# Seven block products instead of eight in the second MLP product of a decoder layer

## The chip, the cores and the metric

The kernel runs on one core of one Trainium2 chip. The core has a matrix engine (TensorE, PE in the profile), a vector engine (VectorE, DVE), a scalar engine (ScalarE, ACT), GpSimd (POOL), and SyncE (SP), whose queue issues nearly all DMA transfers here. The metric is the device time of one execution in microseconds (us). The kernel before takes 924.64 us (median of three runs, 924.51 to 924.73).

## The reference

One layer with two parallel mixers (windowed attention, RWKV-7), a merge, a normalization, and an MLP. All is float32, with 512 tokens of width 1024 after 16 meta tokens are cut off. What matters here are the last lines, where `w_ff1` is 1024 x 4096 and `w_ff2` is 4096 x 1024:

```python
        merged = jax.nn.sigmoid(gate_att) * att + jax.nn.sigmoid(gate_rwkv) * rw
        h = layer_norm(ALPHA * h + merged @ w_out[l], ln1_g[l], ln1_b[l])
        ff = jnp.square(jax.nn.relu(h @ w_ff1[l])) @ w_ff2[l]
        h = layer_norm(ALPHA * h + ff, ln2_g[l], ln2_b[l])
    return h[:, N_META:]
```

## The kernel before

Every float32 product is made of three products of a shorter float type (float32r). An operand is split into `hi`, its rounded copy (a ScalarE cast), and `lo`, the rest (a VectorE subtraction). The three are hi·hi, hi·lo and lo·hi, summed in the same PSUM bank (`three`, L498; `add` in `project`, L1607).

Everything up to the first normalization, and the first three of the 32 up products, is recorded in a plan and issued in a hand-written order of numbers (`ORDER`). The change leaves that order as it is. From L1585 on a scheduler orders the rest by priorities: the code's order counts, but a weight's load, cast and subtraction are moved ahead of it (`load`, L482, `ahead(100)`).

The MLP works on 32 hidden tiles of 128 rows, in two halves of 16 (L1653):

- **Up.** For tile f, `up` (L1664) takes a weight tile of 128 x 1024 (512 KB), splits it into `whi` and `wlo` (L476, L479), and runs 24 matmuls of 512 columns into one PSUM bank: 8 contraction tiles times 3. Their moving operands are the normalized rows `h1hi` and `h1lo`, one row of 512 tokens for each contraction tile. `up_evict` (L1657) makes the ReLU and the square on ScalarE (L1659, L1660), the square once more on VectorE (L1661), and its rest `flo` there too (L1662).
- **Down.** `project` (L1602) is called twice in each half, for output columns 0 to 511 and 512 to 1023. It runs over 16 contraction tiles and 4 blocks of 128 tokens; the stationary operand is a slice of `fhi` or `flo`, the moving one a half of `whi` or `wlo` of 512 columns. Over both halves this is 32 x 4 x 2 x 3 = 768 matmuls. After each call four sums go from PSUM into the residual tiles `res` (L1691).
- **Residual.** `res` holds the normalized rows and is multiplied by `ln1_g` and shifted by `ln1_b` along the way (L1683, eight instructions each, while the up products run).
- **End.** In the last call the four token blocks end one after the other. Each block's sum, statistics (L1631, L1639), root (POOL, L466), two passes of the normalization for each half of the columns (L1598, L1599) and output DMAs (L1647) follow at once; the first half of the columns was added, and its statistics taken, a call earlier.

Of the kernel before, what the change touches and what calls it, by code (L numbers as in the profile page):

```python
# [11 lines left out]
F32 = mybir.dt.float32  # L12
# [71 lines left out]
PRI = {"load": 100}  # L84
HOLD = 4
# [3 lines left out]
SUBST = 1  # L89

# [291 lines left out]
def hybrid_layer_kernel(ctx: ExitStack, tc: tile.TileContext, I: dict, out: bass.AP):  # L382
# [15 lines left out]
    @contextmanager  # L398
    def ahead(n):

        now = tc.cur_priority
        tc.cur_priority = now - n
        yield
        tc.cur_priority += n

# [62 lines left out]

    def split(raw, hi=None, lo=None, n=P):
        if hi is None:  # L470
            hi = wst.tile([P, D], F32R, name="whi", tag="whi", bufs=WB[0])
            lo = wst.tile([P, D], F32R, name="wlo", tag="wlo", bufs=WB[1])
        w = D // 2
        for q in range(2):
            qs = slice(q * w, (q + 1) * w)
            act.copy(hi[:n, qs], raw[:n, qs])  # L476
        for q in range(2):
            qs = slice(q * w, (q + 1) * w)
            dve.tensor_tensor(lo[:n, qs], raw[:n, qs], hi[:n, qs].bitcast(F32), op=ALU.subtract)  # L479
        return hi, lo  # L480

    def load(tiles, i, keep=None):  # L482

        with ahead(PRI["load"]):
            raw = wst.tile([P, D], F32, name="wraw", tag="wraw", bufs=WB[2])
            nc.sync.dma_start(raw, I[tiles][i])
            if keep is None:
                return split(raw)
            return split(
                raw, *(keep.tile([P, D], F32R, name="wk", tag="wk", bufs=2 * (HOLD - 2)) for _ in "hl")  # L490
            )

# [1091 lines left out]
    region.__exit__(None, None, None)  # L1584
    p2.close()  # L1585
    p1.close()
    h1hi, h1lo, fin = fin["hi"], fin["lo"], fin["pool"]
    rp = ctx.enter_context(tc.tile_pool(name="rp", bufs=1, side="right"))
    ffp = ctx.enter_context(tc.tile_pool(name="ffp", bufs=1))

    def rowvec(name, pool_=rp, tag=None):
        t = pool_.tile([P, D], F32, name="rv" + name, tag=tag or "rv" + name[-1], bufs=WB[2] if tag else 1)
        src = I["rows"][ROW0[name] : ROW0[name] + KT].rearrange("(a r) p -> a (r p)", a=1)
        nc.sync.dma_start(t, src.to_broadcast([P, D]))
        return t

    def norm_rows(t, mean, r, g_, b_):
        dve.scalar_tensor_tensor(t, t, mean, g_, op0=ALU.subtract, op1=ALU.mult)  # L1598
        dve.scalar_tensor_tensor(t, t, r, b_, op0=ALU.mult, op1=ALU.add)  # L1599

    res = [[rest_[b, n].t[:, :SEQ] for n in range(2)] for b in range(4)]
    def project(k0, nk, xhi, xlo, n, hold=2, more=None):  # L1602


        acc = [pa.tile([P, 512], F32, name=f"acc{b}", tag=f"acc{b}") for b in range(4)]

        def add(w, q, b):  # L1607
            hi, lo = w
            bs = slice(b * P, (b + 1) * P)
            for d in range(2):  # L1610
                k = q + d
                ws = slice(d * 512, (d + 1) * 512)
                first, last = k == 0, k == nk - 1
                pe.matmul(acc[b], xhi[:, k, bs], hi[:, ws], start=first, stop=False)  # L1614
                pe.matmul(acc[b], xhi[:, k, bs], lo[:, ws], start=False, stop=False)  # L1615
                pe.matmul(acc[b], xlo[:, k, bs], hi[:, ws], start=False, stop=last)  # L1616

        for q in range(0, nk - 2 * hold, 2):
            w = load("w_ff2", k0 + q + n)
            for b in range(4):  # L1620
                add(w, q, b)

        ends = range(nk - 2 * hold, nk, 2)
        ws = [load("w_ff2", k0 + q + n, more if d < hold - 2 else None) for d, q in enumerate(ends)]
        for b in range(4):
            for w, q in zip(ws, ends):
                add(w, q, b)
        return acc

    def half_stats(st, b, n):  # L1630
        dve.bn_stats(st[b][:, n, :], res[b][n])  # L1631

    def stats_tiles():
        return [rp.tile([P, 2, 6], F32, name=f"gst{b}") for b in range(4)]

    def moments(st, b):

        mv = rp.tile([P, 2], F32, name=f"gmv{b}")
        dve.bn_aggr(mv, st[b].rearrange("p a b -> p (a b)"))  # L1639
        return mv[:, 0:1], rstd_of(rp, mv, P, LN_EPS, f"f{b}")  # L1640

    def finish(b):
        mean, r = moments(st2, b)
        for q in range(2):
            qs = slice(q * 512, (q + 1) * 512)
            norm_rows(res[b][q], mean, r, g2[:, qs], b2[:, qs])
            (nc.sync, nc.scalar)[q].dma_start(out[0, b * P : (b + 1) * P, qs], res[b][q])  # L1647

    NF = DFF // P // 2
    taken = [home[id(u.t)] for u in ups]  # L1650
    turn_of = taken + [b for b in banks if b not in taken]
    turn_of = turn_of[: SPLITF] + sorted(turn_of[SPLITF:], key=lambda b: b[0] is pa)[:4]
    for half in range(2):  # L1653
        fhi = ffp.tile([P, NF, SEQ], F32R, name="fhi", tag="fhi")
        flo = ffp.tile([P, NF, SEQ], F32R, name="flo", tag="flo")

        def up_evict(f, ps):  # L1657
            r = rp.tile([P, SEQ], F32, name="rl", tag="rl", bufs=2)
            act.activation(r, ps, AF.Relu)  # L1659
            act.activation(fhi[:, f], r, AF.Square)  # L1660
            dve.tensor_tensor(r, r, r, op=ALU.mult)  # L1661
            dve.tensor_tensor(flo[:, f], r, fhi[:, f].bitcast(F32), op=ALU.subtract)  # L1662

        def up(f, w):  # L1664
            hi, lo = w
            pool_, tag = turn_of[f % len(turn_of)] if half == 0 else (pb, f"acc{f % 4}")
            ps = pool_.tile([P, 512], F32, name="dps", tag=tag)
# [3 lines left out]
            up_evict(f, ps)  # L1671

        split_f = SPLITF if half == 0 else 0
        for f in range(split_f):
            up_evict(f, ups[f].t)
        for f in range(split_f, NF):
            up(f, load("w_ff1", half * NF + f))
            if half == 0 and f in (6, 10):

                gb_ = rowvec(("ln1_g", "ln1_b")[f // 10], wst, "wraw")  # L1680
                for b in range(4):
                    for n in range(2):
                        dve.tensor_tensor(res[b][n], res[b][n], gb_[:, n * 512 : (n + 1) * 512], op=(ALU.mult, ALU.add)[f // 10])  # L1683
        if half == 0:
            g2, b2 = rowvec("ln2_g"), rowvec("ln2_b")
            st2 = stats_tiles()
        for n in range(2):
            ns = slice(n * 512, (n + 1) * 512)
            acc = project(half * NF, NF, fhi, flo, n, HOLD if half and n else 2, ffp)
# [61 lines left out]
```

## Time and profile before

| | before |
|---|---|
| median of three runs | 924.64 us (924.51 to 924.73) |
| profiled execution, first to last instruction (span) | 922.6 us |
| what the runs have around a span like that (924.64 - 922.6) | 2.0 us |
| TensorE busy | 98% of the span, 6496 matmuls |
| weight loads of TensorE | 84% |
| VectorE / ScalarE / GpSimd busy | 63% / 49% / 27% |
| DMA, mean | 104 GB/s |

The page of the profile gives busy times, the busy share in 40 slices of the span, the chain of work that ended last, and groups of equal instructions with the mean duration of one and the idle time ahead of them. A matmul's shown duration is longer than its distance to the next one, since they overlap; what a row of matmuls costs is read from the starts. The timeline lists instructions by start; "x2" means two equal ones that follow each other, with the time from the first start to the last end.

### The profile page before, as it was taken

How to read it: one execution, taken by the hardware profiler on the slowest of the kernel's cores; microseconds unless marked ns; L12 is line 12 of the kernel's file. 1: busy time of each engine (PE TensorE's matmuls, PEld its weight loads, DVE VectorE, ACT ScalarE, POOL GpSimd, SP SyncE). 2: the span in 40 equal slices, each digit the busy share in tenths (PEclk: the TensorE clock that was granted, in tenths of full speed). 3: DMA queues.
4: the chain of work that ended last, by engine and by line, in shares of the span. 5: the costliest groups of instructions: out<-in, count | busy, mean ns of one | idle time of the engine just before them, and what ended most of it. 6: DMA issues, size and time to landing. Idle time of an engine off the chain costs nothing. (4 is left out here: it accounts for less than half of the span.)

```text
span 922.6 us, 17014 instructions
## 1 busy us (share of the span) xinstructions
PE 902.2 (98%) x6496; PEld 773.6 (84%) x6496; DVE 585.8 (63%) x1141; ACT 456.3 (49%) x1080; POOL 245.6 (27%) x652
## 2 busy tenths in 40 slices
PE   7999999999999999999999999999999999999996
PEld 6999989888998888978878878888888888888885
DVE  7873977868777696587685887864323244442437
ACT  7845568476583664656637448434312234431120
POOL 4147173381634605507537020000000000000001
PEclk9999999999999999999989999999999999999999
DMA  7443323425242242313246322532223232233322
GB/s 265 125 131 99 93 84 101 111 67 127 72 110 86 68 141 69 83 54 114 64 140 182 100 92 69 172 126 92 92 91 107 76 114 92 91 93 98 100 75 92
DMA packets 71370, 95.90 MB, mean 104 GB/s; under 512 B 40071, under 2 KB 47497, under 8 KB 71289
## 3 DMA queue, kind: packets, MB, share of 16 engines
q1 hardware_dynamic: 70448, 93.65, 33.5%
q8 instruction: 51, 0.84, 0.4%
q10 hardware_dynamic: 840, 1.17, 0.3%
q14 instruction: 31, 0.25, 0.1%
HBM read 87.64 MB, written 8.21 MB: 104 GB/s over the span
## 5 line engine op out<-in xcount | busy, mean ns | idle before, releaser
L499 PE MATMUL g<-hhi,whi 128*128 128x512 f32 (+3 forms) x640 | 213.1, 333 | 0.2
L500 PE MATMUL g<-hlo,whi 128*128 128x512 f32 (+3 forms) x640 | 204.1, 319 | 1.7 <-DVE hlo L862 1.7
L501 PE MATMUL g<-hhi,wlo 128*128 128x512 f32 (+3 forms) x640 | 203.6, 318 | 0.0
L476 ACT CAST whi<-wraw 128x512 fp32r<-128x512 f32 x118 | 67.4, 619 | 205.7 <-PE acc L1616 107.4
L479 DVE TENSOR_TENSOR wlo<-wraw,whi 128x512 fp32r<-128x512 f32 x118 | 76.4, 689 | 144.5 <-ACT whi L476 141.7
L499 PEld LDWEIGHTS g<-hhi,whi 128*128 128x128 f32 x640 | 121.0, 189 | 12.6 <-issue 2.2
L500 PEld LDWEIGHTS g<-hlo,whi 128*128 128x128 f32 x640 | 121.2, 189 | 9.7 <-DVE hlo L862 2.1
L501 PEld LDWEIGHTS g<-hhi,wlo 128*128 128x128 f32 x640 | 121.0, 189 | 8.5 <-DVE wlo L658 0.2
L658 DVE TENSOR_TENSOR wlo<-wraw,whi 128x512 fp32r<-128x512 f32 x126 | 88.3, 708 | 30.4 <-ACT whi L656 29.8
L1167 POOL TENSOR_TENSOR ftmp<-Xf,Nf 108x84 f32<-108x84 f32 (+23 forms) x248 | 88.1, 355 | 73.4 <-DMA Nf<-Nd 44.7
L656 ACT CAST whi<-wraw 128x512 fp32r<-128x512 f32 x126 | 76.9, 618 | 55.5 <-PE g L500 23.5
L466 POOL TENSOR_TENSOR rsf<-rsf,mhalf 128x1 f32<-128x1 f32 x4 | 3.9, 964 | 348.5 <-DVE rsf L465 348.5
L1171 POOL TENSOR_TENSOR Xf<-Xf,ftmp 108x84 f32<-108x84 f32 (+23 forms) x248 | 88.5, 357 | 19.0
L1615 PE MATMUL acc<-wlo,fhi 128*128 128x512 f32 x240 | 93.4, 389 | 0.0
L1614 PE MATMUL acc<-whi,fhi 128*128 128x512 f32 x240 | 93.4, 389 | 0.0
L1616 PE MATMUL acc<-whi,flo 128*128 128x512 f32 x240 | 93.4, 389 | 0.0
L501 PE MATMUL dps<-h1hi,wlo 128*128 128x512 f32 x232 | 91.6, 395 | 0.0
L499 PE MATMUL dps<-h1hi,whi 128*128 128x512 f32 x232 | 91.6, 395 | 0.0
L500 PE MATMUL dps<-h1lo,whi 128*128 128x512 f32 x232 | 91.6, 395 | 0.0
L1614 PEld LDWEIGHTS acc<-whi,fhi 128*128 128x128 f32 x240 | 45.0, 188 | 9.5
L1616 PEld LDWEIGHTS acc<-whi,flo 128*128 128x128 f32 x240 | 45.0, 188 | 9.3
L1615 PEld LDWEIGHTS acc<-wlo,fhi 128*128 128x128 f32 x240 | 45.0, 188 | 9.3
(361 smaller groups left out, 1658.4 us busy)
## 6 DMA issues: line engine op xcount, KB each, us to landing
wraw<-in_w_ff_dram SPq DMA_DIRECT2D x64, 512.0 KB
wraw<-in_w_in_dram SPq DMA_DIRECT2D x52, 512.0 KB
wraw<-in_w_out_dram SPq DMA_DIRECT2D x14, 256.0 KB
Nf<-Nd SPq DMA_DIRECT2D x24, 144.0 KB
res<-in_x_dram SPq DMA_DIRECT2D x4, 512.0 KB
G<-in_consts_dram SPq DMA_DIRECT2D x16, 128.0 KB
XB<-xtd SPq DMA_DIRECT2D x16, 128.0 KB
res<-in_x_dram SPq DMA_DIRECT2D x8, 256.0 KB
```

What stands on the lines that cost most here:

```text
L476: act.copy(hi[:n, qs], raw[:n, qs])
L479: dve.tensor_tensor(lo[:n, qs], raw[:n, qs], hi[:n, qs].bitcast(F32), op=ALU.subtract)
L499: pe.matmul(ps, whi, xhi, start=first, stop=False)
L500: pe.matmul(ps, whi, xlo, start=False, stop=False)
L501: pe.matmul(ps, wlo, xhi, start=False, stop=last)
L656: AC(512, lambda hi=hi, qs=qs: act.copy(hi.t, raw.t[:, qs]), plain=True, r=[raw], w=[hi], new=[hi])
L658: f = lambda hi=hi, lo=lo, qs=qs, e=e: e.tensor_tensor(lo.t, raw.t[:, qs], hi.t.bitcast(F32), op=ALU.subtract)
L1167: sub(nj * nt, lambda s=s, nj=nj, nt=nt, tv=tv: pool.tensor_tensor(tv(), Xf.t[:, 0:nj, s : s + 1].to_broadcast([NB, nj, nt]), Nf.t[:, s : ...
L1171: sub(nj * nt, lambda s=s, nj=nj, tv=tv: pool.tensor_tensor(Xf.t[:, 0:nj, s + 1 :], Xf.t[:, 0:nj, s + 1 :], tv(), op=ALU.add), port=1, r=[ ...
L1614: pe.matmul(acc[b], xhi[:, k, bs], hi[:, ws], start=first, stop=False)
L1615: pe.matmul(acc[b], xhi[:, k, bs], lo[:, ws], start=False, stop=False)
L1616: pe.matmul(acc[b], xlo[:, k, bs], hi[:, ws], start=False, stop=last)
```

## The change

The second MLP product is cut into four groups of 8 hidden tiles. In three of them (24 of the 32 tiles, 12 of 16 pairs) each group is a 2 x 2 times 2 x 2 product of blocks: tokens 0 to 255 or 256 to 511 (t), even or odd tiles of the group (x), and output columns 0 to 511 or 512 to 1023 (d). Instead of eight block products of 24 matmuls there are seven, with sums of weight blocks and differences of activation blocks made on VectorE; several products go on in the same two PSUM banks (a chain, R, T or P), and after each the chain's present value is added to or taken from a quarter of `res`. The last group keeps eight products, in eight units.

The order is now the code's own, for the whole MLP. The list of units alternates one up product and one of the seven, and the last group's units end it. For unit i the loads are issued four units ahead, the splits (`prep`) two units ahead, then its matmuls, then its follow-up (`post`). The three up products of the plan are evicted ahead of the first unit. The square is made by VectorE alone, in place, and split when it is used. `res` gets the factor ALPHA with `ln1_g` and `ln1_b` in two lots of eight VectorE instructions, behind units 2 and 3. `finish` takes both halves' statistics at the end. A pad is 128 B longer: `h1hi` and `h1lo` began 128 B past a multiple of 512 B, and now begin at one. The weights of the second product lie in host memory in quarters of 1 MB, and one quarter of each of the three groups is loaded twice.

```diff
-        fin["pad"] = p.tile([P, 88], F32, name="fpad")
+        fin["pad"] = p.tile([P, 120], F32, name="fpad")
...
+    def finish(b, g2, b2):
+        for n in range(2):
+            dve.bn_stats(st2[b][:, n, :], res[b][n])
...
+        for q in range(2):
+            qs = slice(q * 512, (q + 1) * 512)
+            dve.scalar_tensor_tensor(res[b][q], res[b][q], mv[:, 0:1], g2[:, qs], op0=ALU.subtract, op1=ALU.mult)
+            dve.scalar_tensor_tensor(res[b][q], res[b][q], r, b2[:, qs], op0=ALU.mult, op1=ALU.add)
+            (nc.sync, nc.scalar)[q].dma_start(out[0, b * P : (b + 1) * P, qs], res[b][q])
...
+    bank_of = {"u": free[:2], "R": free[2:4], "P": [free[4], taken[0]], "T": taken[1:3]}
...
+        pool_, n = {"w": (wst, WB[0]), "b": (mp, 3), "a": (mp, 2)}[kind]
+        return tuple(pool_.tile([P, D], F32R, name=kind + q, tag=kind + q, bufs=n) for q in ("hi", "lo"))
...
+    def up_evict(f, ps):
+        t = ff_of(f // NF)[:, f % NF]
+        act.activation(t, ps, AF.Relu)
+        dve.tensor_tensor(t, t, t, op=ALU.mult)
...
+    def split_left(src):
+        hi, lo = pair_of("a")
+        v = lambda t: t.rearrange("p (i c) -> p i c", c=256)
+        act.copy(v(hi), src)
+        dve.tensor_tensor(v(lo), src, v(hi).bitcast(F32), op=ALU.subtract)
+        return hi, lo
+
+    def split_right(t):
+        out = []
+        for c in range(NP // 2):
+            hi, lo = pair_of("bw"[c % 2])
...
+    def products(left, right, acc, bs, first, last, again=False):
+        (ahi, alo) = left
+        for b in bs:
+            for i in range(NP):
+                bhi, blo = right[i // 2]
+                as_ = slice(i * 256 + b * P, i * 256 + (b + 1) * P)
+                ws = slice((i % 2) * 512, (i % 2 + 1) * 512)
+                for q, (l, r) in enumerate(((ahi, bhi), (ahi, blo), (alo, bhi))):
+                    pe.matmul(acc[b], l[:, as_], r[:, ws], start=first and i == 0 and q == 0,
+                              stop=last and i == NP - 1 and q == 2, skip_group_check=True)
...
+    def down(g, n):
+        left, chain, updates = (
+            ((1, 0),                 "R", (2, 0, ALU.add)),
+            (((1, 1), (1, 0)), "T", (2, 0, ALU.add)),
+            (((0, 1), (1, 0)), "R", (2, 1, ALU.subtract)),
+            ((0, 1),                 "P", (0, 1, ALU.add)),
+            (((1, 0), (0, 0)), "R", (0, 1, ALU.subtract)),
+            (((1, 1), (0, 1)), "P", (2, 1, ALU.add)),
+            (((0, 0), (0, 1)), "R", (0, 0, ALU.add)),
+        )[n]
+        first = n in (0, 1, 3)
+        loads = [[load_raw(g, 0, 0), load_raw(g, 1, 0)], [], [load_raw(g, 0, 1)], [load_raw(g, 1, 1)], [], [], [load_raw(g, 0, 0)]][n]
...
+            if n == 0:
+                chains["sum"] = plus(x0, y0)
+            elif n == 2:
+                plus(chains["sum"], x1)
+            elif n == 3:
+                plus(chains["sum"], y1)
+            elif n == 6:
+                plus(x0, x1)
+            right = (chains["sum"], y0, chains["sum"], chains["sum"], x1, y1, x0)[n]
+            if isinstance(left[0], tuple):
+                src = mp.tile([P, NP, 256], F32, name="dif", tag="dif", bufs=2)
+                dve.tensor_tensor(src, block_of(g, *left[0]), block_of(g, *left[1]), op=ALU.subtract)
...
+            s["r"] = split_right(right)
+            s["l"] = split_left(src)
...
+        def post():
+            b, d, op = updates
+            for i in range(2):
+                dve.tensor_tensor(res[b + i][d], res[b + i][d], chains[chain][i], op=op)
...
+        return [
+            unit(0, 0, (0,), both, [load_raw(g, 0, 0), load_raw(g, 0, 1)], [(0, 0)], [(0, 0)]),
+            unit(1, 0, (0,), both, [load_raw(g, 1, 0), load_raw(g, 1, 1)], [(1, 0)]),
...
+            unit(0, 1, both, (0,), (), [(0, 1)], [(1, 0)], done(0, 0)),
+            unit(0, 1, both, (1,), (), [], (), done(0, 1)),
+            unit(1, 1, both, (0,), (), [(1, 1)], (), done(1, 0)),
+            unit(1, 1, both, (1,), (), (), (), done(1, 1)),
+        ]
...
+    units = [up(f) for f in range(SPLITF, NF)]
+    units[1].loads.append(first_rows)
+    for i, k in ((2, 0), (3, 1)):
+        was = units[i].post
+        units[i].post = lambda was=was, k=k: (was(), scaled(None, k)())
+    for g in range(NG - 1):
+        f = (g + 1) * NF
+        for n in range(7):
+            units.append(up(f))
+            f += 1
+            if n == 3:
+                units.append(up(f))
+                f += 1
+            units.append(down(g, n))
+    units += last_group(NG - 1)
+    for f in range(SPLITF):
+        up_evict(f, ups[f].t)
+    for i in range(-LEAD[0], len(units)):
+        if 0 <= i + LEAD[0] < len(units):
+            for f in units[i + LEAD[0]].loads:
+                f()
+        if 0 <= i + LEAD[1] < len(units):
+            units[i + LEAD[1]].prep()
+        if i >= 0:
+            units[i].run()
+            units[i].post()
```

Three places show what this does to the instruction order.

**Entry, ScalarE.** Where the MLP begins, before: `h1hi` is the last of the normalized rows, `g` a PSUM bank of one of the plan's three up products, `wraw` a weight tile.

```order
L1557 CAST h1hi<-e_132 128x4x128
L476 CAST whi<-wraw 128x512 x4
L1659 ACTIVATE rl<-g 128x512 x2
L1660 ACTIVATE fhi<-rl 128x512 x2
L476 CAST whi<-wraw 128x512 x2
L1659 ACTIVATE rl<-g 128x512
```

The same place now (`up` is the bank of a later up product):

```order
L1524 CAST h1hi<-e_132 128x4x128
L1604 ACTIVATE ff<-g 128x512 x3
L1618 CAST whi<-wraw 128x1024 x3
L1604 ACTIVATE ff<-up 128x512
L1618 CAST whi<-wraw 128x1024
```

The casts of the next weights stood ahead of the evictions of the three banks, and stand behind all three now.

**First product, VectorE.** Around the scaling of `res` (res_125 to res_128 are its tiles), before:

```order
L1683 TENSOR_TENSOR res_126<-res_126,rvln_g 128x512
L1661 TENSOR_TENSOR rl<-rl 128x512
L1683 TENSOR_TENSOR res_127<-res_127,rvln_g 128x512
L1662 TENSOR_TENSOR flo<-rl,fhi 128x512
L1683 TENSOR_TENSOR res_125<-res_125,rvln_g 128x512
L479 TENSOR_TENSOR wlo<-wraw,whi 128x512 x2
```

Now, from the end of the second lot of eight to the second product's difference (`braw` is a quarter of the weights, or a sum of quarters):

```order
L1771 SCALAR_TENSOR_TENSOR res_127<-rows_6740,res_127 128x512
L1771 SCALAR_TENSOR_TENSOR res_125<-rows_6740,res_125 128x512
L1685 TENSOR_TENSOR braw<-braw 128x2048
L1653 TENSOR_TENSOR blo<-braw,bhi 128x1024
L1653 TENSOR_TENSOR wlo<-braw,whi 128x1024
L1644 TENSOR_TENSOR alo<-ff,ahi 128x1024
L1605 TENSOR_TENSOR ff<-ff 128x512
L1619 TENSOR_TENSOR wlo<-wraw,whi 128x1024
L1605 TENSOR_TENSOR ff<-ff 128x512
L1701 TENSOR_TENSOR dif<-ff 128x1024
```

The scaling was spread between other work; it now stands in two closed lots, and the operands of the first of the seven products come behind the second lot.

**Last group, VectorE.** Before, ahead of the last call's four blocks:

```order
L1691 SCALAR_TENSOR_TENSOR res_127<-res_127,acc_8406 128x512
L479 TENSOR_TENSOR wlo<-wraw,whi 128x512 x2
L1631 BN_STATS gst_7264<-res_127 128x6
L479 TENSOR_TENSOR wlo<-wraw,whi 128x512 x2
L479 TENSOR_TENSOR wk<-wraw,wk 128x512 x4
L479 TENSOR_TENSOR wlo<-wraw,whi 128x512 x4
```

Now, where the last group begins (`dnR` are chain R's two banks, which the last group's first product uses again; `alo` is the rest of an activation block, first of block (0, 0), then of block (1, 0)):

```order
L1653 TENSOR_TENSOR blo<-braw,bhi 128x1024
L1653 TENSOR_TENSOR wlo<-braw,whi 128x1024
L1644 TENSOR_TENSOR alo<-ff,ahi 128x1024
L1605 TENSOR_TENSOR ff<-ff 128x512
L1644 TENSOR_TENSOR alo<-ff,ahi 128x1024
L1715 TENSOR_TENSOR res_126<-res_126,dnR 128x512
L1715 TENSOR_TENSOR res_128<-res_128,dnR 128x512
```

The two additions that empty chain R stand behind the split of block (1, 0), whose `ahi` and `alo` take the buffer that the seventh product has just read.

More of the change, by code (lines that the diff above doesn't have):

```diff
@@ L89 @@
 SUBST = 1
+NG = 4
+LEAD = (4, 2)
 ORDER = [
@@ L1602, in project @@
[L1602 to L1628, printed above, removed]
@@ L1647, in finish @@
             (nc.sync, nc.scalar)[q].dma_start(out[0, b * P : (b + 1) * P, qs], res[b][q])
-    NF = DFF // P // 2
     taken = [home[id(u.t)] for u in ups]
[L1651 to L1667, printed above, removed]
+    free = [b for b in banks if b not in taken]
```

192 lines of the change are left out of this document (112 added, 80 removed).

## The prediction

> **What bounds the kernel now.** First the page's busy times and its chain of the work that ended last, shares by engine:
>
> ```profile
> span 922.6 us, 17014 instructions
> PE 902.2 (98%) x6496; PEld 773.6 (84%) x6496; DVE 585.8 (63%) x1141; ACT 456.3 (49%) x1080; POOL 245.6 (27%) x652
> PE 38%; DVE 1%; issue 1%; ACT 0%; POOL 0%; DVEq 0%; POOLq 0%
> ```
>
> The change touches the MLP alone, so second the view by windows over it (window; its length, busy time and count of TensorE; then weight loads, VectorE, ScalarE, GpSimd; granted clock; DMA share; GB/s): first half's up products, its down products, and the same of the second half.
>
> ```profile
> 580.00:650.00 70.00, 70.00 (x301) 56.31 (x300) 45.30 (x71) 29.43 (x52) 0.00 (x0) 1.00 0.38 122
> 652.00:736.00 84.00, 84.00 (x373) 69.54 (x372) 24.82 (x39) 16.97 (x30) 0.00 (x0) 1.00 0.29 94
> 740.00:826.00 86.00, 86.00 (x371) 69.17 (x370) 40.56 (x61) 34.05 (x60) 0.00 (x0) 1.00 0.32 101
> 830.00:913.00 83.00, 83.00 (x368) 68.73 (x367) 35.65 (x60) 14.85 (x26) 2.87 (x3) 1.00 0.28 89
> ```
>
> TensorE has no idle time in any of the four, at full clock, and the weights come at about a third of what the DMA engines could give. So the MLP's time is matmuls times their distance, plus its end. Third the timeline, for that distance: every sixth of a row, first up, then down.
>
> ```profile
> 634.64 0.39 PE L499 MATMUL dps<-h1hi,whi 128*128 128x512 f32 x1
> 636.04 0.39 PE L499 MATMUL dps<-h1hi,whi 128*128 128x512 f32 x1
> 699.72 0.39 PE L1614 MATMUL acc<-whi,fhi 128*128 128x512 f32 x1
> 701.08 0.39 PE L1614 MATMUL acc<-whi,fhi 128*128 128x512 f32 x1
> ```
>
> An up matmul takes 1.40 / 6 = 0.2333 us, a down matmul 1.36 / 6 = 0.2267 us. The shapes are equal. What differs is the moving operand: `h1hi` and `h1lo` begin 128 B past a multiple of 512 B, the weight halves at one.
>
> **What is removed.** Down matmuls: 768 before; now three groups of 7 x 24 = 504 and a last one of 8 x 24 = 192, together 696. The 72 fewer save 72 x 0.2267 = 16.3 us. Alignment: 29 up products of 24 matmuls, 696 x 0.0067 = 4.6 us if the operand's start is the reason; bounds 0 and 4.6 (the shorter up matmuls of the plan have the same operand and could give a little more; taken at 0). I take 4.6, since the two rows differ in nothing else that I see. Together 20.9 us.
>
> On this the Trainium skill has a rule, on its page "SBUF — State Buffer", section "Specifications (TRN2)": lines of 16 bytes, at least two hits on each for full bandwidth. A shift by 128 B moves no element to another place in such a line, so by it the 4.6 us would be 0; the rows 0.2333 and 0.2267 speak against it but don't show the cause.
>
> **What is added beside TensorE's work.** The prices of the wide operations, from the timeline: two casts and two subtractions that follow each other, three products into `res`, and two weight loads on SyncE's queue; then the group of the narrowest two-operand form, 256 columns:
>
> ```profile
> 605.91 1.15 ACT L476 CAST whi<-wraw 128x512 fp32r<-128x512 f32 x2 [3.29 <-PE dps L500]
> 607.08 1.29 DVE L479 TENSOR_TENSOR wlo<-wraw,whi 128x512 fp32r<-128x512 f32 x2
> 610.69 1.89 DVE L1683 TENSOR_TENSOR res<-res,rvln_b 128x512 f32<-128x512 f32 x3
> 592.05 3.34 SPq L486 DMA_DIRECT2D wraw<-in_w_ff_dram  x2
> L1090 DVE TENSOR_TENSOR GR<-g,con 64x256 f32<-64x256 f32 x32 | 13.5, 420 | 0.9 <-PE g L1076 0.3
> ```
>
> Two operands of 512 columns go at 0.60 us each, so 1024 columns take about 1.2, and 2048 about 2.4. A cast of 1024 takes 1.0 to 1.15. A steady group has 8 up products and 7 block products, 15 x 24 x 0.2267 = 81.6 us. VectorE in it: 8 ups at 1.2 for the rest and 0.6 for the square, 14.4; 7 products at three splits and two additions, 7 x 4.8 = 33.6; 5 differences, 6.0; 4 sums, 9.6: 63.6 us, 78%. If the differences and the activations' splits, which read stretches of 256, cost 4 x 0.42 = 1.68 instead of 1.2, it is 69.4. ScalarE: 8 x 1.7 + 7 x 3 = about 35 us. The tightest pair, a product with sum and difference beside an up product, has 10.2 us of VectorE in 10.9. Operands are prepared two units ahead, so this stays hidden: 0. Loads are asked four units, 21 us, ahead, and 1 MB came in 3.34 us: 0 for the 3 MB loaded twice. The square leaves ScalarE and stays on VectorE, the old `flo` goes: counted above.
>
> **Four waits that are new.** They are where the lead of two units isn't there yet, or the order stands in its way.
>
> *Entry.* The last matmuls of the plan and what ScalarE does beside them:
>
> ```profile
> 577.43 1.09 ACT L1659 ACTIVATE rl<-g 128x512 f32<-128x512 f32 x2 [0.40 <-PE g L501]
> 577.82 0.28 PE L501 MATMUL g<-h1hi,wlo 128*128 128x256 f32 x1
> 577.94 0.40 PE L499 MATMUL dps<-h1hi,whi 128*128 128x512 f32 x1
> ```
>
> Today the first weights are cast before the evictions and the next up product starts at 577.94, without a gap. Now three evictions at 0.50 stand ahead of the cast: 577.43 + 1.5 = 578.93, and the cast ends at about 580.05. That is 2.1 us late. The first two matmuls need `whi` alone; the third needs `wlo`, 1.2 us behind the cast, less 0.45: 0.8. I take **2.9** (bounds 2.1 and 2.9).
>
> *First block product.* Let E be the end of the third new up product, whose follow-up carries the first eight scalings of `res`. What these cost, and the ReLU, I read here and in the kernel's last microseconds, which the tail needs too:
>
> ```profile
> 591.12 0.59 ACT L1659 ACTIVATE rl<-dps 128x512 f32<-128x512 f32 x1
> 914.38 0.24 PE acc L1616
> 914.64 0.69 DVE L1691 SCALAR_TENSOR_TENSOR res<-res,acc 128x512 f32<-128x512 f32 x1 [0.94 <-PE acc L1616]
> 915.36 0.69 DVE L1631 BATCH_NORM_STATS2 gst<-res 128x6 f32<-128x512 f32 x1
> 916.09 0.21 DVE L1639 BATCH_NORM_AGGREGATE gmv<-gst 128x2 f32<-128x12 f32 x1
> 916.33 0.15 DVE L465 TENSOR_SCALAR rsf<-gmv 128x1 f32<-128x1 f32 x1
> 916.40 1.40 DVE L1598 SCALAR_TENSOR_TENSOR res<-res,gmv,rvln_g 128x512 f32<-128x512 f32 x2
> 916.57 0.99 POOL L466 TENSOR_TENSOR rsf<-rsf,mhalf 128x1 f32<-128x1 f32 x1 [4.45 <-DVE rsf L465]
> 917.73 1.41 DVE L1599 SCALAR_TENSOR_TENSOR res<-res,rsf,rvln_b 128x512 f32<-128x512 f32 x2
> ```
>
> Two instructions of the scalings' kind (L1598) take 1.40 together and 0.74 the one, so eight take 8 x 0.66 = 5.3. VectorE from E: ReLU 0.6, square 0.6, eight scalings, to E + 6.5; rest of an up product, 7.7; square and the second eight, 13.6; sum of two quarters, 16.0. Three casts of about 1.05 follow on ScalarE, the activations' last: E + 19.1. TensorE has three up products of 5.44 in between and would start at E + 16.2. It waits 2.9, then after two matmuls another 1.3 for the activations' rest, behind two weight subtractions in VectorE's queue (E + 20.8): **4.2** (bounds 2.9 and 4.7, the latter with 1.68 for the rest). Who waits behind the closed lots is the up product's rest alone, and it is two units early.
>
> *Last group.* Its second product needs `ahi` of block (1, 0), in the buffer that the seventh product reads until its end: + 0.2 for the last matmul's own time, the cast 1.1. Its first product, block (0, 0), starts only once chain R's banks are empty, and those two additions stand behind that block's rest on VectorE: the cast, 1.2 for the rest, 0.7 for the addition, and small steps: 0.2 + 1.1 + 1.2 + 0.7 = **3.2** (bounds 2.4, if the scheduler lets the first addition go ahead of part of it, and 3.7).
>
> *Tail.* Each of the last four units ends a block, 5.44 us of TensorE. Its work on VectorE, by the rows above: two additions 1.20, statistics 0.60 + 0.73, aggregate 0.24, root until the second pass 1.40 (916.33 to 917.73), then second pass, first pass of the other half, second pass, 0.66 + 0.78 + 0.66: 6.26. VectorE falls behind from the first block's end: 5.66 + 3 x 6.26 + 0.1 = 24.5 us later, which is 24.5 - 16.3 = 8.2 behind TensorE's end. Before, that was 914.61 to 917.73 + 1.41 = 919.14, 4.5. The last DMA's 922.6 - 919.1 = 3.5 stays. **3.7** (bounds 3.0 and 4.2).
>
> Together 2.9 + 4.2 + 3.2 + 3.7 = 14.0; with 20.9 removed, -6.9.
>
> **The clock.** TensorE's waits can cost more than their length. Once before, in a sparse stretch of the plan:
>
> ```profile
> 462.00:464.00 2.00, 0.67 (x7) 0.35 (x6) 1.91 (x4) 0.26 (x1) 0.00 (x0) 1.00 0.60 232
> 464.00:466.00 2.00, 1.41 (x50) 1.18 (x52) 1.94 (x6) 1.17 (x3) 0.00 (x0) 0.71 0.34 47
> 466.00:471.70 5.70, 5.59 (x70) 4.87 (x64) 4.53 (x10) 2.98 (x7) 0.64 (x1) 0.50 0.67 205
> 463.61 0.24 PE L1191 MATMUL g<-U,NT 32*32 32x32 f32 x2 [1.18 <-DVE U L1198]
> ```
>
> With TensorE busy 0.67 of 2 us the clock fell to a half: (1 - 0.71) x 2 / 0.5 = 1.2 us and then 5.7 us, about 6.9 us. In the MLP such a spell loses 3.4 us of work. The first block product's wait, 4.2 us with two matmuls in it, is emptier than that stretch, so I expect a fall there; whether it lasts the whole spell depends on where it falls, and I take half, **+1.7** (bounds 0 and 3.4). Entry (2.9) and last group (3.2) are about as empty but shorter: 0 taken, 3.4 each as the far bound. Sum: -6.9 + 1.7 = -5.2; the profiled span would be 917.3, and 2.0 around it give 919.3.
>
> **The rivals.**
> 1. *Alignment buys nothing* and the 0.2333 has another reason (the stationary operand's way into the array, say). For it: no trace shows the same product at both places. 919.3 + 4.6 = 923.9, no change by measure. Chance 0.10; the rule on 16-byte lines above gives this time.
> 2. *VectorE late in the seven products.* If the wide operations cost 30% more than their width says, a group's VectorE work is 63.6 x 1.3 = 82.7 against 81.6: 1.1 for each of three groups, and 1.5 more in the first product's chain: about +4.8, 924.1. From some 28% on VectorE is the bound. Against it: additions follow each other at 0.60 with no gain or loss for width to be seen. Chance 0.08.
> 3. *Slower: the clock falls in each of three waits*, entry, first product and last group, for a whole spell. 3 x 3.4 = 10.2; -6.9 + 10.2 = +3.3, 927.9. It decides once all three fall, since two give -0.1. For it: the row of 462 needed no longer emptiness than 1.2 us at a time. Against: two of the waits are broken by matmuls or lie beside full stretches. Chance 0.08.
> 4. *The clock never falls*, 917.6. Chance 0.12. The Trainium skill, page "TensorE: Matmul & The Clock Gate", section "What's actually happening", has the half clock only behind at least one idle window of about 3.4 us; by it none of these waits costs more than its length. The fall at 464 without so long an idle time speaks against that.
> 5. The change does what it says: the instruction order has the 72 matmuls fewer, so no chance is kept for that.
>
> **How the numbers follow.** Forecast 919.3, chance 0.62. The range reaches down to 915.0, rival 4 with some 2.6 of the waits' lower ends, and up to 924.2, which takes in rivals 1 and 2 and the forecast with one more spell (922.7). A measurement of this kernel tells about 0.2%, 1.85 us, from no change: faster is under 922.8, slower above 926.5. Faster: forecast and rival 4, and a part of rival 2, 0.76; same: rival 1 and the rest of rival 2, 0.16; slower: rival 3, 0.08.
>
> **What would show it.** Right: up matmuls at 0.2267 like the down ones; no gap in TensorE between the first product's start and the last group's; gaps of about 2.1 + 0.8 at 578, 2.9 + 1.3 some 30 us later, 3.2 before the last group, and 8.2 us from the last matmul to VectorE's last instruction; a stretch at granted clock 0.5 behind the second gap. Wrong: up matmuls still at 0.2333, idle TensorE within the groups with VectorE as the releaser, half clock in several places, or gaps that aren't there since the operands were ready.

## The result and the profile after

The changed kernel takes 918.94 us (median of four runs, 918.13 to 919.94) beside 924.58 for the kernel before; the ratio is 0.9942, with a 95% interval from 0.9929 to 0.9954. That is 5.6 us faster; 919.3 was forecast. The profiled execution spans 916.4 us, 6.2 less than before.

The page, in the lines that answer to those of before: busy times, and the chain that ended last. VectorE has gone from 63% to 73%, and TensorE has now 1% less of its span.

```profile
span 916.4 us, 16744 instructions
PE 885.1 (97%) x6424; PEld 761.2 (83%) x6424; DVE 668.6 (73%) x1152; ACT 471.1 (51%) x1030; POOL 245.8 (27%) x652
PE 32%; DVE 4%; issue 1%; ACT 1%; POOL 0%; POOLq 0%; DVEq 0%
```

There are 6496 - 6424 = 72 matmuls fewer. The view by windows (columns as in the prediction) cuts the MLP where TensorE's busy time falls short of the window's length: entry, first block product, the three groups, the last group's start, the end.

```profile
577.50:584.00 6.50, 4.41 (x14) 2.97 (x14) 4.26 (x5) 3.37 (x5) 0.00 (x0) 0.74 0.26 69
614.00:621.50 7.50, 4.95 (x15) 3.36 (x14) 6.96 (x8) 6.20 (x8) 0.00 (x0) 0.77 0.10 13
625.00:856.00 231.00, 231.00 (x1021) 191.28 (x1020) 174.11 (x170) 93.96 (x105) 0.00 (x0) 1.00 0.35 122
857.00:862.00 5.00, 2.14 (x10) 1.51 (x9) 2.38 (x4) 3.45 (x4) 0.00 (x0) 1.00 0.00 1
905.00:916.00 11.00, 0.38 (x2) 0.00 (x0) 7.52 (x13) 0.00 (x0) 0.99 (x1) 0.63 0.25 95
```

The three groups run without a gap, with VectorE busy for 174.1 of 231 us (75%; 78% was worked out). The time lies in three places, 577, 614 and 857, where the clock fell at the first two (0.74 and 0.77 in the mean), and in the end. The timeline at the three places, with what released the matmuls (in square brackets: the idle time of the engine and the instruction that ended it):

```profile
577.81 0.28 PE L468 MATMUL g<-h1hi,wlo 128*128 128x256 f32 x1
579.97 0.62 PE L466 MATMUL up<-h1hi,whi 128*128 128x512 f32 x1 [1.88 <-ACT whi L1618]
614.41 0.39 PE L468 MATMUL up<-h1hi,wlo 128*128 128x512 f32 x1
616.44 0.50 PE L1665 MATMUL dnR<-bhi,ahi 128*128 128x512 f32 x1 [1.64 <-ACT ahi L1643]
618.09 0.79 PE L1665 MATMUL dnR<-bhi,alo 128*128 128x512 f32 x1 [0.91 <-DVE alo L1644]
858.35 0.39 PE L1665 MATMUL dnR<-whi,alo 128*128 128x512 f32 x1
858.55 1.04 ACT L1643 CAST ahi<-ff 128x1024 fp32r<-128x1024 f32 x1 [4.61 <-PE dnR L1665]
859.62 1.23 DVE L1644 TENSOR_TENSOR alo<-ff,ahi 128x1024 fp32r<-128x1024 f32 x1 [3.82 <-ACT ahi L1643]
860.77 1.28 DVE L1715 TENSOR_TENSOR res<-res,dnR 128x512 f32<-128x512 f32 x2
861.59 0.47 PE L1665 MATMUL last<-bhi,ahi 128*128 128x512 f32 x1 [2.86 <-ACT whi L1652]
```

The last five are read from top to bottom: the seventh product ends, the cast gets its buffer, the rest, the two additions that empty chain R, and at the end of the first of them the last group starts. The profile names a cast (`whi`) as the releaser of 861.59; the addition that ends some 0.1 us before is the one that experiment 7 bears out.

The tail: TensorE's last matmul and VectorE's last instruction.

```profile
904.99 0.39 PE L1665 MATMUL last<-whi,alo 128*128 128x512 f32 x1
912.35 0.75 DVE L1573 SCALAR_TENSOR_TENSOR res<-res,rsf,rows 128x512 f32<-128x512 f32 x1
```

VectorE ends 913.10 - 905.38 = 7.7 us behind TensorE (8.2 forecast, 4.5 before).

Where the time went. A wait is the time between two matmuls' starts beyond 0.2267 us; a half clock's loss is the sum of what the matmuls around it start later than that, less the waits (the granted clock was at a half for (1 - 0.74) x 6.5 / 0.5 = 3.4 us in the entry's window, and for as long in the first product's):

| | forecast | profiled execution |
|---|---|---|
| 72 matmuls fewer, up matmuls at 0.2267 (by the distances) | -20.9 | -20.9 |
| entry, waits | 2.9 | 1.9 + 0.6 = 2.5 |
| first block product, waits | 4.2 | 1.8 + 1.1 = 2.9 |
| last group, wait | 3.2 | 3.1 |
| tail | 3.7 | 7.7 - 4.5 = 3.2 |
| half clock | 1.7 | 1.4 at the entry + 1.6 at the first product = 3.0 |
| sum | -5.2 | -6.2 |

The last sum is the difference of the spans (916.4 - 922.6).

### The profile page after: what moved, and what is told of

It is laid out like the page before. It is cut to its first block, busy times and chain, and to the rows that moved or that the text cites. A ratio compares the mean times of both kernels' runs of the same rounds, so it can differ in the third digit from the quotient of the medians.

```text
span 916.4 us, 16744 instructions
## 1 busy us (share of the span) xinstructions
PE 885.1 (97%) x6424; PEld 761.2 (83%) x6424; DVE 668.6 (73%) x1152; ACT 471.1 (51%) x1030; POOL 245.8 (27%) x652
## 5 line engine op out<-in xcount | busy, mean ns | idle before, releaser
L625 DVE TENSOR_TENSOR wlo<-wraw,whi 128x512 fp32r<-128x512 f32 x126 | 88.5, 709 | 30.4 <-ACT whi L623 29.7
L623 ACT CAST whi<-wraw 128x512 fp32r<-128x512 f32 x126 | 76.9, 618 | 55.6 <-PE g L467 23.9
L466 PE MATMUL up<-h1hi,whi 128*128 128x512 f32 x232 | 91.0, 392 | 1.9 <-ACT whi L1618 1.9
L468 PE MATMUL up<-h1hi,wlo 128*128 128x512 f32 x232 | 90.9, 392 | 0.2 <-DVE wlo L1619 0.2
L467 PE MATMUL up<-h1lo,whi 128*128 128x512 f32 x232 | 90.8, 391 | 0.0
L1652 ACT CAST bhi<-braw 128x1024 fp32r<-128x1024 f32 x25 | 26.2, 1049 | 61.1 <-DVE braw L1685 53.1
L466 PEld LDWEIGHTS up<-h1hi,whi 128*128 128x128 f32 x232 | 43.8, 189 | 11.0 <-ACT whi L1618 2.1
L468 PEld LDWEIGHTS up<-h1hi,wlo 128*128 128x128 f32 x232 | 43.8, 189 | 10.1 <-DVE wlo L1619 0.9
L467 PEld LDWEIGHTS up<-h1lo,whi 128*128 128x128 f32 x232 | 43.9, 189 | 9.1
L1618 ACT CAST whi<-wraw 128x1024 fp32r<-128x1024 f32 x29 | 30.3, 1048 | 23.2 <-PE dnR L1665 12.0
```

Source lines behind the costliest of these rows:

```text
L466: pe.matmul(ps, whi, xhi, start=first, stop=False)
L467: pe.matmul(ps, whi, xlo, start=False, stop=False)
L468: pe.matmul(ps, wlo, xhi, start=False, stop=last)
L623: AC(512, lambda hi=hi, qs=qs: act.copy(hi.t, raw.t[:, qs]), plain=True, r=[raw], w=[hi], new=[hi])
L625: f = lambda hi=hi, lo=lo, qs=qs, e=e: e.tensor_tensor(lo.t, raw.t[:, qs], hi.t.bitcast(F32), op=ALU.subtract)
L1618: act.copy(hi, s["raw"])
```

## The experiments

All times are medians; the changed kernel (918.94) is the base unless another is named. The kernel before was timed beside each lot of experiments: 924.58 beside the changed kernel, 924.54 with experiments 1 to 4, 924.14 with 5 to 8, 923.68 with 9 to 12. So a difference between lots carries a drift of up to 0.9 us. Experiments 1 and 2 tell the pad's gain from that of the seven products.

**1, the pad alone undone.** In the changed kernel:

```diff
-        fin["pad"] = p.tile([P, 120], F32, name="fpad")
+        fin["pad"] = p.tile([P, 88], F32, name="fpad")
```

> The changed kernel with the pad at its old length, so that the normalized rows begin 128 B past a multiple of 512 B again; nothing else differs. Theory (the start of the moving operand sets 0.2267 or 0.2333 us for one matmul): up matmuls at 0.2333, 696 x 0.0067 = 4.6 us more, 923.5 us. Rival (the new order or the new kinds of products made the up matmuls faster): they stay at 0.2267 and the time at 918.9.

Measured 923.06 us, +4.1. The up matmuls' starts, first of the changed kernel, then of this one, each six matmuls apart:

```profile
636.21 0.39 PE L466 MATMUL up<-h1hi,whi 128*128 128x512 f32 x1
637.57 0.39 PE L466 MATMUL up<-h1hi,whi 128*128 128x512 f32 x1
```

```profile
636.80 0.40 PE L466 MATMUL up<-h1hi,whi 128*128 128x512 f32 x1
638.19 0.40 PE L466 MATMUL up<-h1hi,whi 128*128 128x512 f32 x1
```

1.36 / 6 = 0.2267 against 1.39 / 6 = 0.2317; over the up matmuls of this kernel's trace behind the entry the mean is 0.2328. The theory holds, a little under its size. The pad moves `h1hi`, `h1lo` and a few small tiles of VectorE; the weights and the PSUM banks of the up matmuls stay where they were, so for these matmuls the moving operand's place is all that differs.

**2, the pad alone made**, in the kernel before (the same two lines the other way).

> The kernel before with the longer pad alone. Theory: its up matmuls fall from 0.2333 to 0.2267 and the time by 4.6 to 5.3 us (the upper end if the 144 short up matmuls of the plan gain as well), to 919.3 to 920.0: nearly all of what the whole change gave, since the 72 matmuls saved are spent on the new waits. Rival: 924.6, no change.

Measured 919.99 us, 4.6 less than before (924.54 in these runs; ratio 0.9958, 0.9946 to 0.9969). In the view by groups its up matmuls have the same 389 ns as its down matmuls:

```profile
L1614 PE MATMUL acc<-whi,fhi 128*128 128x512 f32 x240 | 93.4, 389 | 0.0
L500 PE MATMUL dps<-h1lo,whi 128*128 128x512 f32 x228 | 88.7, 389 | 0.0
```

So 128 bytes of padding alone give 4.6 of the 5.6 us. The seven products, as they are ordered here, give what is left: about 1, or 1.5 by the two ratios (0.9958 and 0.9942).

**3, eight products in the new order.** In the first three groups each block product by itself, no sums or differences:

```diff
-        for n in range(7):
+        for n in range(8):
             units.append(up(f))
             f += 1
-            if n == 3:
-                units.append(up(f))
-                f += 1
             units.append(down(g, n))
...
-        left, chain, updates = (...)[n]
+        t, d, x = n // 4, n // 2 % 2, n % 2
+        chain = "RT"[d]
...
+            s["r"] = split_right(raws[g, x, d])
+            s["l"] = split_left(block_of(g, t, x))
```

> The changed kernel with eight block products instead of seven in the first three groups too, in the same alternating order with the same lead, without sums, differences or sign changes (one product more per group, no quarter loaded twice). Theory (TensorE's count decides, the additions on VectorE are hidden within the groups): 72 matmuls more, +16.3 us; the first product needs no sum of quarters, so its wait of 2.9 us and the half clock behind it (1.65) go or shrink: 931 to 935 us. Rival (the seven products' additions cost TensorE time that the eight don't): below 928.

Measured 927.56 us, +8.6. That is under the 928 set for the rival, but the view of waits shows why, and it isn't the rival's reason:

```profile
PE up L466 <- ACT whi L1618: 1.9, 1, 1.9
PE up L468 <- DVE wlo L1619: 0.5, 1, 0.5
```

These are all of TensorE's waits in its MLP. The first product's are gone, as expected, and the last group's too, which the expectation missed: the last two of the eight products use chain T, so R is empty in time. 16.3 - 4.5 (first product with its half clock) - 3.1 = 8.7. So the time alone would not have told theory from rival here; the waits do.

**4, the waits filled.** Matmuls on data at hand, into empty banks, where TensorE would wait; nothing reads them:

```diff
+    def warm(key, j, n):
+        ps = psum(key, j, "warm")
+        for k in range(n):
+            pe.matmul(ps, h1hi[:, k, :P], h1hi[:, k], start=k == 0, stop=k == n - 1, skip_group_check=True)
...
+            if i in (0, 6):
+                warm("RT"[i // 6], 0, (8, 7)[i // 6])
             units[i].run()
```

and three and four more ahead of the third matmul of each.

> The changed kernel with 22 matmuls that compute nothing (moving h1hi, into banks that are empty then) put into the waits of TensorE at the entry (8, then 3 ahead of the third matmul) and at the first block product (7, then 4). The waits stay. Theory (an empty stretch lets the clock fall, and a half clock lost 1.36 us at the entry and 1.65 us at the first product in the profiled run): no half clock behind either, 3.0 us less, 915.9. Rival 1 (the falls come by a phase of their own): half clock as before, 918.9. Rival 2 (the waits are set by something that the filling matmuls delay): up to 1 us more than that.

Measured 916.65 us, 2.3 less. The windows are entry and first product, then two stretches of 3.41 us at the start of the last group, whose wait was left as it is:

```profile
577.50:584.00 6.50, 6.46 (x31) 4.92 (x30) 4.26 (x5) 3.40 (x5) 0.00 (x0) 1.00 0.26 80
614.00:621.50 7.50, 7.44 (x32) 5.51 (x32) 7.50 (x8) 6.17 (x8) 0.00 (x0) 1.00 0.22 68
856.49:859.90 3.41, 0.82 (x4) 0.72 (x5) 2.78 (x4) 3.41 (x5) 0.00 (x0) 1.00 0.00 0
859.90:863.31 3.41, 3.41 (x10) 2.63 (x9) 3.41 (x4) 0.97 (x2) 0.00 (x0) 0.50 0.00 0
```

The clock stays whole where the waits are filled: in the profiled execution the entry and the first product end 2.5 us earlier. It fell at the unfilled wait at the last group, for 3.4 us, which takes 1.6 us of that back. It had not fallen there in the changed kernel's profile, though the wait is the same 3.0 us:

```profile
856.67:860.08 3.41, 2.06 (x10) 1.37 (x8) 0.46 (x1) 1.53 (x2) 0.00 (x0) 1.00 0.03 11
860.09:863.50 3.41, 1.91 (x8) 1.61 (x9) 3.41 (x5) 3.30 (x4) 0.00 (x0) 1.00 0.00 0
```

The clock records of the traces show what differs. In each of the 14 profiles all changes of the clock lie whole multiples of 3.413 us apart, on a grid whose place differs from execution to execution; the four windows just shown are cut at it. In experiment 4 one cell of the grid takes in most of the wait, and the next cell runs at a half; in the changed kernel the wait is divided between two cells, and neither is followed by a half clock. Over the MLPs of all 14 profiles, up to their last matmul, each of the 15 full-clock cells in which TensorE was busy for at most 1.52 us was followed by a fall, three of five between 1.53 and 1.76, and none with more. (This bound is for these matmuls of 512 columns: among the smaller ones ahead of the MLP cells fell that were busy for 2 us and more.) So both theory and rival 1 have a part: emptiness makes the fall, and the grid's place decides whether one cell gets enough of it.

**5, 6, 7 and 8, one edit for each wait.** The entry: evictions behind the casts.

```diff
-    for f in range(SPLITF):
-        up_evict(f, ups[f].t)
     for i in range(-LEAD[0], len(units)):
+        if i == 0:
+            for f in range(SPLITF):
+                up_evict(f, ups[f].t)
```

> The changed kernel with the three evictions of the plan's up products issued behind the casts of the first two new weight tiles instead of ahead of them. Theory (the entry's wait is the casts' place behind the evictions): the 2.5 us of waits at 578 go, and the half clock behind them (1.4 us in the profiled run): 3.9 less, 915.0 us. Rival (the casts then wait for the weights' transfer or for their buffers): part of the wait stays, 916 to 919.

Measured 913.97 (911.65 to 917.22), 5.0 less, or 4.5 with the drift of 0.4 taken off. The entry's window has no gap and the whole clock, which is the 3.9 expected; the rest is within that spread:

```profile
577.50:584.00 6.50, 6.50 (x31) 5.43 (x30) 3.53 (x5) 2.94 (x6) 0.00 (x0) 1.00 0.51 164
```

The first product's operands: scalings spread.

```diff
-    for i, k in ((2, 0), (3, 1)):
+    for i, bs, n in ((2, (2, 3), 0), (4, (2, 3), 1), (5, (0, 1), 1), (7, (0, 1), 0)):
         was = units[i].post
-        units[i].post = lambda was=was, k=k: (was(), scaled(None, k)())
+        units[i].post = lambda was=was, bs=bs, n=n: (was(), scaled(bs, n)())
```

> The changed kernel with the sixteen scalings of the residual tiles spread over four units (each tile's product and sum together, the tiles in the order in which the seven products first use them) instead of in two closed lots. Theory (the first block product's operands are late since they stand behind the second lot on VectorE): the waits of 2.9 us and the half clock behind them (1.65 us) go: 4.5 less, 914.4. Rival (what is late is the sum of quarters and three casts, or the quarters' transfer): more than 1.5 us of the wait stays, 916 to 919, or new waits at the next products.

Measured 916.39, 2.6 less (2.1 without the drift) where 4.5 was expected. The first product and the last group's start:

```profile
610.00:618.00 8.00, 8.00 (x37) 6.64 (x36) 7.93 (x11) 5.07 (x7) 0.00 (x0) 1.00 0.01 2
857.00:862.00 5.00, 4.19 (x12) 3.37 (x13) 5.00 (x7) 2.60 (x3) 0.00 (x0) 0.66 0.00 0
```

The wait is gone whole, and in the profiled execution the first product ends 4.6 us earlier for it. Two other things took some of that: the clock fell at 857, (1 - 0.66) x 5 / 0.5 = 3.4 us, a loss of 1.6, and the entry ended 0.8 later, ahead of the place where the edit acts. 4.6 - 1.6 - 0.8 = 2.2, the difference of the spans.

The last group: another bank.

```diff
-        ... psum(*[("R", i), ("T", i), ("P", i), ("u", i)][2 * t + d], "last")
+        ... psum(*[("T", i), ("R", i), ("P", i), ("u", i)][2 * t + d], "last")
```

> The changed kernel with the last group's first product in chain T's banks instead of chain R's (and the fourth one in R's). Theory (the last group's first matmul waits for the additions that empty R, and these for the split of block (1, 0) ahead of them on VectorE, whose buffer the seventh product reads): the 3.1 us at 858 go, 915.8 us; the split of block (1, 0) has a whole unit of 5.4 us then. Rival (the first matmul waits for its own operand): nothing, or one wait a unit later.

Measured 914.66, 4.3 less (3.8 without the drift), with nothing left of the wait. The spans of the profiled executions, 916.4 and 912.5, differ by 3.9: 3.1 at the last group, as expected, and 0.7 to 0.8 that is there from the entry on, ahead of the place where the edit acts:

```profile
856.00:862.00 6.00, 6.00 (x29) 4.95 (x28) 3.04 (x4) 4.13 (x5) 0.00 (x0) 1.00 0.01 5
```

So the first matmul's own operands were not what it waited for.

The end: both first passes ahead of both second ones.

```diff
         for q in range(2):
             qs = slice(q * 512, (q + 1) * 512)
             dve.scalar_tensor_tensor(res[b][q], res[b][q], mv[:, 0:1], g2[:, qs], ...)
+        for q in range(2):
+            qs = slice(q * 512, (q + 1) * 512)
             dve.scalar_tensor_tensor(res[b][q], res[b][q], r, b2[:, qs], ...)
```

> The changed kernel with the first passes of both halves ahead of both second passes in the end of each block, so that the second half's first pass lies in the wait for GpSimd's root. Theory (VectorE's work of 6.3 us a block against 5.44 of TensorE adds up over four blocks): 0.7 to 0.75 less a block, so 5.55 a block: 4 blocks in all 2.9 less, 916.0. Rival (only the last block's order counts, since VectorE keeps up with the first three): 0.7 less, 918.2.

Measured 915.87, 3.1 less (2.6 without the drift). Its last matmul and last pass:

```profile
904.63 0.39 PE L1667 MATMUL last<-whi,alo 128*128 128x512 f32 x1
908.71 1.41 DVE L1575 SCALAR_TENSOR_TENSOR res<-res,rsf,rows 128x512 f32<-128x512 f32 x2
```

VectorE ends 910.12 - 905.02 = 5.1 us behind TensorE, 2.6 less than 7.7. That is far more than the one block's 0.7, so the four blocks' delays do add up.

**9, all four.**

> The changed kernel with all four edits: evictions behind the first casts, scalings spread, the other bank for the last group's first product, first passes ahead of second ones. Theory (the four costs stand apart): 3.9 + 4.5 + 3.1 + 2.9 = 14.4 less, 904.5 us, TensorE without a gap from 578 to its last matmul and no half clock in between. Rival (some of them hide each other or a new wait takes their place): above 907.

Measured 903.26 us (901.76 to 904.97); to the kernel before in those runs (923.68) the ratio is 0.9779, 0.9766 to 0.9792. That is 15.7 us less than the changed kernel, 14.8 without the drift, where 14.4 was expected; the rival, above 907, falls. TensorE has no gap and the whole clock from the entry to its end:

```profile
577.50:584.00 6.50, 6.50 (x31) 5.35 (x30) 3.90 (x6) 2.94 (x5) 0.00 (x0) 1.00 0.47 161
608.00:621.00 13.00, 13.00 (x59) 10.78 (x58) 12.86 (x17) 4.61 (x6) 0.00 (x0) 1.00 0.14 41
625.00:845.00 220.00, 220.00 (x972) 182.08 (x971) 169.62 (x166) 92.46 (x103) 0.00 (x0) 1.00 0.35 123
850.00:892.00 42.00, 42.00 (x187) 34.79 (x186) 27.75 (x41) 8.24 (x9) 2.97 (x3) 1.00 0.07 26
```

**10, the four edits with eight products** (experiment 3's edit on top, and the scalings in the order in which the eight use the tiles).

> The four edits with eight block products instead of seven in the first three groups as well (the scalings in the order in which the eight use the tiles). Theory: 72 matmuls and nothing else, 16.3 us more than the four edits with seven: 920.8 us, about that of the kernel before with the longer pad alone (920.0). Rival (the seven's sums and differences cost TensorE something that shows only here): less than 15 us more, under 919.5.

Measured 924.92 us, 21.7 more, where 16.3 was expected. The other bank is the wrong one here: the eight end in chain T, so experiment 7's edit gives the last group the bank that is emptied last.

```profile
866.00:871.00 5.00, 2.14 (x10) 1.44 (x9) 3.52 (x5) 4.60 (x5) 0.00 (x0) 0.98 0.02 3
871.00:874.00 3.00, 3.00 (x9) 2.32 (x8) 3.00 (x4) 0.25 (x1) 0.00 (x0) 0.50 0.00 0
```

That wait, 3.1, and the half clock behind it, 1.6, make up 4.7 of the 5.4 us too much; the rest is within the spread of the medians. The theory and the rival both missed that wait, but it shows the bank's part a second time, with the roles of R and T exchanged. Without the 4.7 the eight products would take about 920.2 us, which is an estimate; the kernel before with the longer pad took 919.99. As far as that estimate goes, the new order and the four edits give next to nothing by themselves, and what experiment 9 gains beyond the pad is the 72 matmuls.

**11, more work on VectorE**, on top of the four edits:

```diff
+            more = mp.tile([P, 512], F32, name="more", tag="more", bufs=1)
+            for i in range(NP):
+                dve.tensor_tensor(more, right[:, i], right[:, i], op=ALU.add)
             s["r"] = split_right(right)
```

> The four edits, and in the preparation of each of the 21 products four more additions of 512 columns on VectorE, whose result nothing reads: about 2.3 us a product, 16 a group, so that VectorE is busy for about 78 of a group's 81.6 us. Theory (only a group's total counts, since a lead of two units smooths the rest): as the four edits, within 2 us. Rival (the tightest pair counts: product with sum and difference beside an up product, 10.2 + 2.3 = 12.5 us of VectorE in 10.9 of TensorE): 1.6 us or more for two products of each group, and the half clock where they are empty enough: 10 us or more.

Measured 914.97 us, 11.7 more: the theory that only the total counts falls. The windows, first products and the rest:

```profile
615.00:641.00 26.00, 21.50 (x85) 16.54 (x84) 25.66 (x32) 8.03 (x9) 0.00 (x0) 0.93 0.23 81
641.00:850.00 209.00, 206.37 (x910) 170.26 (x909) 199.76 (x220) 82.80 (x93) 0.00 (x0) 1.00 0.33 115
```

Most of it, 7.2 us of lost time, lies at the first two products, where the scalings share VectorE, and where operands are late: the rests made on VectorE, above all.

```profile
PE dnR L1667 <- DVE alo L1646: 1.8, 1, 1.8
PE dnT L1667 <- DVE alo L1646: 1.8, 1, 1.8
```

From 641 on VectorE is 96% busy and TensorE misses only 2.6 us in 209, once in each of two groups. One of these places:

```profile
700.06 1.28 DVE L1720 TENSOR_TENSOR res<-res,dnR 128x512 f32<-128x512 f32 x2
700.89 0.47 PE L1667 MATMUL dnR<-bhi,ahi 128*128 128x512 f32 x1 [1.31 <-DVE res L1720]
```

The operands are ready there; late is the addition that lets chain R's bank go. So the rival's size is right, but its reason is not: behind the first two products the tightest pairs wait for no operands, and it is not two products of each group that are late.

**12, a lead of one unit**, on top of the four edits:

```diff
-LEAD = (4, 2)
+LEAD = (4, 1)
```

> The four edits with the operands prepared one unit ahead instead of two (loads four ahead as before). Theory (the way from the sum or difference through the casts to the first matmul is longer than one unit of 5.44 us): each product with a sum or a difference starts late, 0.5 to 4 us each, 20 to 60 us in all with the clock: 925 to 965. Rival (one unit suffices): as the four edits.

Measured 939.9 us, 36.6 more. TensorE's waits, summed by what ended them (us, times, longest):

```profile
PE dnR L1667 <- ACT ahi L1645: 8.2, 9, 3.8
PE dnR L1667 <- DVE alo L1646: 7.9, 9, 0.9
PE dnP L1667 <- ACT ahi L1645: 3.5, 3, 1.2
PE dnP L1667 <- DVE alo L1646: 2.7, 3, 0.9
```

Twelve of the 21 products show in this view, each late first for the activations' cast, then for their rest. The time is within the 925 to 965 expected; that every product with a sum or a difference comes late, which is all 21, this view does not show.

## Why the prediction was right, step by step

- **The bound.** TensorE's matmuls times their distance: right. The three groups have no gap.
- **Alignment, 4.6 us.** Right, and shown from both sides: undone +4.1, alone -4.6. Rival 1 falls. The Trainium skill's lines of 16 bytes ("SBUF — State Buffer", "Specifications (TRN2)") give no difference for a shift by 128 B; the measured 0.2328 and 0.2267 us disagree with that reading.
- **Matmuls, 16.3 us.** Right: eight products cost 8.6 more, and 8.7 by that count with the waits that they avoid; in experiment 10 21.7 more, of which 4.7 is the wrong bank, so 17.0.
- **Entry, 2.9.** 2.5 in waits; the mechanism is shown by experiment 5.
- **First product, 4.2.** 2.9. The mechanism is shown by experiment 6, the size was too large: eight scalings took 4.9 us each lot instead of 5.3, the sum 2.29 instead of 2.4, and the three casts followed each other at 0.95 instead of 1.05. The rows:

```profile
599.76 4.90 DVE L1771 SCALAR_TENSOR_TENSOR res<-res,rows 128x512 f32<-128x512 f32 x8
606.31 4.91 DVE L1771 SCALAR_TENSOR_TENSOR res<-rows,res 128x512 f32<-128x512 f32 x8
611.12 2.29 DVE L1685 TENSOR_TENSOR braw<-braw 128x2048 f32<-128x2048 f32 x1
```

- **Last group, 3.2.** 3.1, as said, link by link.
- **Tail, 3.7.** 3.2; the mechanism is shown by experiment 8.
- **Clock, 1.7.** 3.0 in the profiled execution. Here the term was mis-sized in two ways that partly cancel: each fall lasted 3.4 us, not the 6.9 of the plan's, and there was one at the entry, where 0 was taken. That the first product's fall cost 1.6, near the 1.7 taken, is luck: half of a spell of 6.9 us was meant, and the whole of one half as long came. The three waits and the tail were taken 2.3 us too large together, the clock 1.3 too small; that the sum came so near is in part luck too.
- **Rival 2** (VectorE late) didn't come: 75% busy. Experiment 11 shows that at 96% within the groups the bank's release is what comes late.
- **Rivals 3 and 4** put the clock at all or none. Both are off: a fall costs 1.4 to 1.6 us, so three would cost about 4.8, not 10.2, and the change would still have been faster. Nor does it never fall: the rule of the Trainium skill ("TensorE: Matmul & The Clock Gate", "What's actually happening") with an idle window of about 3.4 us would keep the clock whole here, but it fell with no idle time above 1.9 us, and filling the waits kept it whole.

So a wait of 3 us brings a half clock in some executions and none in others, by its place in the grid of 3.413 us, which no edit here sets. The runs of one kernel fit this: in experiment 5 the granted clock over the whole run was 0.992 at 911.65 and 912.60 us, 0.990 at 913.97 and 914.06, and 0.986 at 917.22. What stays open is why busier cells fell too among the smaller matmuls ahead of the MLP.

## What to carry to other kernels

A change that saves a bounding engine's work is worth what its edges leave of it: beside the pad, 16.3 us of matmuls gave 1 to 1.5 here, and about 16 (919.99 to 903.26 is 16.7, with a drift of 0.9) once four costs at the first and last units of a smooth schedule were taken out, by edits of a few lines. Look at the place where a new steady state begins and ends: what stands ahead of the first operand, which bank or buffer the next stage takes first, and what is emptied last. And test a cheap part of a change (here a pad) alone: it may be most of the gain.

## What the runs showed that was not expected

- A moving operand that begins 128 B past a multiple of 512 B costs 6 to 7 ns for each matmul of 512 columns (0.2328 to 0.2333 against 0.2267 us), 4 to 5 us for this kernel. The runs compare these two places only; other offsets weren't tried.
- The half clock came in spells of 3.4 us (once 6.8, in experiment 12) in the MLP, also behind waits of 2 to 3 us, always on a grid of 3.413 us and behind a cell in which TensorE was busy for at most 1.76 us; in the changed kernel each spell took 1.4 to 1.6 us.
- The name of a releaser can mislead: the last group's first matmul was put down to a cast, and the bank decided.
